# Transformer block on one core: one 512-column product for both activation parts in every transposed-output stage

## The chip, the cores and the metric

One Trainium2 chip, one of its cores. The metric is the device time of one execution in microseconds (us). Engines go by the names of the profile: PE (TensorE), with its weight loads as PEld, DVE (VectorE), ACT (ScalarE), POOL (GpSimd), SP (SyncE, which here only issues DMA).

## The reference

One block over 256 rows of width 1024, in f32. h is an RMS norm of x; `h @ w_in` (2048 columns) gives four 512-wide pieces: the input u of a pooling mixer, and q, k, v of an attention with 8 heads of 64 (RMS norm by head, rope, causal). Their outputs side by side go through `w_out` and are added to x. A second norm feeds a cross attention with 4 heads of 256 to a 256-row memory (`w_xq`, `w_xkv`, `w_xo`), added to x again. Last comes a gated feed-forward with a causal convolution of width 3:

```python
x = x + jnp.concatenate([pool, attn], axis=-1) @ w_out[l]
h = _rms_norm(x, norm_xattn_g[l]); m = _rms_norm(mem, norm_mem_g[l])
x = x + _cross_attention(h, m, w_xq[l], w_xkv[l], xq_norm_g[l], xk_norm_g[l], w_xo[l])
h = _rms_norm(x, norm_ffn_g[l])
up = h @ w_up                                   # 5632 columns: gate and val
up = sum_j conv_w[j] * shift(up, 2 - j) + conv_b
x = x + (silu(up[..., :2816]) * up[..., 2816:]) @ w_down
```

## The kernel before, in words

**Two parts for each operand.** Every f32 operand of a large product is split in a high part (ACT rounds it to f32r) and a low part (DVE subtracts the high part from the value). A product is then three products of f32r: high by high, low activation by high weight, high activation by low weight. Weights come from HBM in 62 chunks of 128 x 2048 (1 MB), each two *units* of 128 x 1024; `need(u)` issues `split_h` (ACT, `wh`, L194) and `split_l` (DVE, `wl`, L205) for units ahead of the one that PE is about to use, by `LOOKS` units (4 in most stages). Buffers are rings: `raw` 3 chunks, `wh` 7 units, `wl` 6.

**Two kinds of stage.** In `a_chunk` the activation is the stationary operand and 512 weight columns move; each 128-deep block k makes six products of 512 columns (L366, L367, L370). There are eight such chunks: k, q, v, u of `w_in` and four of `w_xkv`. The other stages give a transposed output: `b_tile` makes an output tile f of 128 features by 256 rows, with a 128 x 128 weight block as the stationary operand and the 256 activation columns moving. For each block k, `three` issues three products of 256 columns (L265, L266, L267). These stages are `w_out` (stage h1), `w_xq` (xq), `w_xo` (h2), `w_up` (up: 22 iterations i of a gate tile and a value tile) and `w_down` (down): 8 units each for the first three, 44 and 22 for the last two, so 90 units of 8 blocks, 720 calls of `three`.

**Emptying a tile.** In `resid_stage` (h1, h2) DVE adds the PSUM tile to the residual (L719), ACT writes the high part of the result times a gain (`part_h`, L250), DVE the low part (`part_l`, L256), ACT squares it (L725) and POOL sums the squares (L726). In xq the parts are made straight from PSUM. In up, `up_job` takes the two tiles of one bank: ACT writes y = conv_w[2] * tile + b (L896, two halves), DVE adds the two shifted taps (L903, four instructions), ACT Silu (L907), DVE gate times value (L909), ACT high part (L248), DVE low part (L254). In down DVE adds the residual (L946) and SP stores the tile.

**The last norm.** The first iterations of up multiply the unnormalised h2 and scale the result afterwards by r2b (L891, `SCALED` = 4 iterations). Meanwhile `r2_job` sums the squares over rows on PE (L281), makes 1/sqrt by Newton steps on POOL (`rsqrt`, L226 on DVE, then L228 to L231 three times on POOL), spreads it over partitions on PE (L869), copies it (r2b, L871, DVE) and makes hs = h2 * r2 block by block (L881, POOL), with its high part on ACT and low part on DVE. From i = 4 on PE multiplies hs.

**Rope and scores.** `rope_table` (L382, POOL) makes cos and sin times the gain of the q or k norm. `rope` on DVE multiplies with it (m1 L404, m2 L408), sums squares (L411) and adds (L413). `qk_job` then makes 1/rms of every head (`head_scale`: DVE `hk`/`hq` L243, then `rsqrt`, mostly on POOL), multiplies k by it (L431), and transposes on PE (L438). For q the scale is kept apart (`sp`, `sneg`, L445, L446, POOL) and is used in `score_job` (L530, L536).

**The order of the work** is written out by the program: jobs are generators, `tick()` advances each one by a step, and `tick()` is called after every second `three` inside `b_tile` (twice a block in `a_chunk`). `WAIT_...` lists say how many ticks a job lets pass before its next instruction is issued. Each engine then runs its own queue strictly in the order of issue, and waits where an input is not there.

Of the kernel before, what the change touches and what calls it, by code (L numbers as in the profile page):

```python
# [76 lines left out]
def block_kernel(ctx: ExitStack, tc: tile.TileContext, wpack: bass.AP, xpack: bass.AP, scal: bass.AP,  # L77
# [268 lines left out]
    xgv = tiles(pair("xg"))  # L346
# [354 lines left out]
    def b_tile(u0, f, blocks, b, mov):  # L701

        for k in range(blocks):
# [8 lines left out]
    def resid_stage(u0, actv, gain, name, phase, held):  # L712
        hv = tiles(pair(name))
        acc = t1(name + "_acc")
        for f in range(KT):
# [1 line left out]
            look[0] = HOLD[2] if f >= KT - HOLD[held] else LOOKS[phase]
            b_tile(u0, f, KT, b, lambda k: [t[:, k] for t in actv])
            dve.tensor_tensor(resid[:, f], b, resid[:, f], op=ALU.add)  # L719
            evac_split(hv[0][:, f], hv[1][:, f], resid[:, f], col(sc, gain + f))  # L720
# [24 lines left out]
    def x_job(hp):  # L745
# [56 lines left out]
    jobs_x = []  # L802
    for f in range(KT):
        b = bank()[:, 0:S]
        b_tile(34, f, KT, b, lambda k: [t[:, k] for t in h1])
        if f == 0:
            job_r1.append(go(r1_job()))
# [239 lines left out]
```

## Time and profile before

| what | value |
|---|---|
| time, three runs | 394.35, 394.62, 396.85 us; median 394.62 |
| the profiled execution | 395.07 us, span of its instructions 393.3 us |
| busy PE / DVE / ACT / POOL | 387.0 / 283.1 / 231.5 / 90.0 us |
| moved by DMA | 69.2 MB, mean 176 GB/s |

Busy time of an engine is the union of its instructions; PE's matmuls overlap one another, so the distance between two starts, not the duration of one, is what a product costs. In a timeline a row may stand for several instructions in succession (x4); the bracket is the time for which the engine sat idle before the row, and what ended that.

### The profile page before, as it was taken

To read this page: it belongs to the slowest core of one execution; us is meant where nothing else is said; L and a number is where in the kernel's file an instruction comes from. 1 tells how busy PE (TensorE), PEld (TensorE's weight loads), DVE (VectorE), ACT (ScalarE), POOL (GpSimd) and SP (SyncE) were. 2 spreads that over 40 slices of the span, in tenths; PEclk is the share of its full clock that TensorE was granted. 3 is DMA by queue.
4 is the path that set the end of the run, shared out by engine and by line. 5 is a ranking of instruction groups with operands and counts; after the bars stand their busy time and mean duration, and the time that the engine had idled before them with its cause. 6 is when DMAs were issued, how large, how long until landed. Compare 5 with 4: busy or idle time off the path is not lost.

```text
span 393.3 us, 7301 instructions
## 1 busy us (share of the span) xinstructions
PE 387.0 (98%) x2898; PEld 367.2 (93%) x2898; DVE 283.1 (72%) x478; ACT 231.5 (59%) x421; POOL 90.0 (23%) x174
## 2 busy tenths in 40 slices
PE   8999999999999999999999999999999999999996
PEld 7878787889999998899999999999999999999996
DVE  4788989956876667857774999998877874543350
ACT  5775886957476556845555498765665576342300
POOL 0384883134441423001647300000000000000000
PEclk9999999999999999999999999999999999999999
DMA  8985372543336537242545226665465452455400
GB/s 273 422 342 207 119 304 72 166 190 108 109 107 222 208 107 262 76 198 107 202 143 197 105 108 227 243 249 177 176 213 180 161 197 108 135 227 176 173 21 19
DMA packets 12274, 69.22 MB, mean 176 GB/s; under 512 B 1360, under 2 KB 2768, under 8 KB 4688
## 3 DMA queue, kind: packets, MB, share of 16 engines
q1 hardware_dynamic: 11952, 68.24, 47.9%
q8 instruction: 22, 0.36, 0.4%
q10 hardware_dynamic: 288, 0.52, 0.4%
q14 instruction: 12, 0.10, 0.1%
HBM read 67.71 MB, written 1.05 MB: 175 GB/s over the span
## 4 chain that ended last, share of the span: by engine, by line
PE 80%; DVE 7%; DMA 5%; ACT 3%; POOL 2%; issue 2%; SPq 0%; DVEq 0%; POOLq 0%
PE bank L265 23%; PE bank L267 23%; PE bank L266 23%; DMA raw<-wpack 3%; PE bank L366 3%; PE bank L367 3%; PE bank L370 3%; DVE wl L205 2%; DMA sc<-xpack 1%; ACT wh L194 1%; DVE mg_l L256 1%; ACT sqx L300 0%; PE bank L677 0%; PE bank L795 0%; POOL rs3t L228 0%
## 5 line engine op out<-in xcount | busy, mean ns | idle before, releaser
L205 DVE TENSOR_TENSOR wl<-raw,wh 128x1024 fp32r<-128x1024 f32 (+1 forms) x126 | 150.3, 1209 | 5.4 <-ACT wh L194 5.3
L194 ACT CAST wh<-raw 128x1024 fp32r<-128x1024 f32 (+1 forms) x125 | 123.7, 1024 | 41.6 <-DMA raw<-wpack 41.0
L265 PE MATMUL bank<-hs_h,wh 128*128 128x256 f32 x288 | 81.5, 283 | 0.0
L266 PE MATMUL bank<-hs_l,wh 128*128 128x256 f32 x288 | 81.5, 283 | 0.0
L267 PE MATMUL bank<-hs_h,wl 128*128 128x256 f32 x288 | 81.5, 283 | 0.0
L265 PEld LDWEIGHTS bank<-hs_h,wh 128*128 128x128 f32 x288 | 55.3, 192 | 0.0
L266 PEld LDWEIGHTS bank<-hs_l,wh 128*128 128x128 f32 x288 | 55.3, 192 | 0.0
L267 PEld LDWEIGHTS bank<-hs_h,wl 128*128 128x128 f32 x288 | 55.3, 192 | 0.0
L265 PE MATMUL bank<-act_h,wh 128*128 128x256 f32 x176 | 49.8, 283 | 0.0
L266 PE MATMUL bank<-act_l,wh 128*128 128x256 f32 x176 | 49.8, 283 | 0.0
L267 PE MATMUL bank<-act_h,wl 128*128 128x256 f32 x176 | 49.8, 283 | 0.0
L903 DVE SCALAR_TENSOR_TENSOR y<-bank,sc,y 128x255 f32<-128x255 f32 (+1 forms) x72 | 29.8, 479 | 14.4 <-ACT y L896 14.4
L265 PE MATMUL bank<-h_h,wh 128*128 128x256 f32 x128 | 36.6, 286 | 0.0
L267 PE MATMUL bank<-h_h,wl 128*128 128x256 f32 x128 | 36.2, 283 | 0.0
L266 PE MATMUL bank<-h_l,wh 128*128 128x256 f32 x128 | 36.2, 283 | 0.0
L896 ACT ACTIVATE y<-bank,sc 128x256 f32<-128x256 f32 x36 | 18.3, 559 | 27.6 <-PE bank L267 27.6
L265 PEld LDWEIGHTS bank<-act_h,wh 128*128 128x128 f32 x176 | 33.8, 192 | 0.0
L266 PEld LDWEIGHTS bank<-act_l,wh 128*128 128x128 f32 x176 | 33.8, 192 | 0.0
L267 PEld LDWEIGHTS bank<-act_h,wl 128*128 128x128 f32 x176 | 33.8, 192 | 0.0
L946 DVE TENSOR_TENSOR o<-bank,sc 128x256 f32<-128x256 f32 x8 | 3.4, 425 | 35.2 <-PE bank L267 35.2
L366 PE MATMUL bank<-wh,mg_h 128*128 128x512 f32 x64 | 26.1, 408 | 0.0
L726 POOL TENSOR_TENSOR h_acc<-h_sq,h_acc 128x256 f32<-128x256 f32 x14 | 16.8, 1198 | 40.3 <-ACT h_sq L725 40.2
(244 smaller groups left out, 862.4 us busy)
## 6 DMA issues: line engine op xcount, KB each, us to landing
raw<-wpack SPq DMA_DIRECT2D x59, 1024.0 KB, 4.8
raw<-wpack SPq DMA_DIRECT2D x4, 512.0 KB, 7.7
mraw<-memT SPq DMA_DIRECT2D x4, 256.0 KB, 7.7
out<-o SPq DMA_DIRECT2D x8, 128.0 KB, 1.9
raw<-wpack ACTq DMA_DIRECT2D x2, 256.0 KB, 3.7
raw<-wpack SPq DMA_DIRECT2D x2, 256.0 KB, 4.7
sc<-xpack SPq DMA_DIRECT2D x1, 512.0 KB, 6.0
tab<-table SPq DMA_DIRECT2D x1, 480.0 KB, 9.7
```

The source lines that it names most:

```text
L194: copy(split[u][0][:, r], unit(u)[:, r])
L205: dve.tensor_tensor(l[:, r], unit(u)[:, r], h[:, r].bitcast(F32), op=ALU.subtract)
L256: dve.scalar_tensor_tensor(l, src, scale, h.bitcast(F32), op0=ALU.mult, op1=ALU.subtract)
L265: pe.matmul(o, stat[0], mov[0], start=start, stop=False)
L266: pe.matmul(o, stat[0], mov[1], start=False, stop=False)
L267: pe.matmul(o, stat[1], mov[0], start=False, stop=stop)
L366: pe.matmul(bk[tt], a[tt][0], wv[0], start=k == 0, stop=False)
L367: pe.matmul(bk[tt], a[tt][1], wv[0], start=False, stop=False)
L370: pe.matmul(bk[tt], a[tt][0], wv[1], start=False, stop=k == KT - 1)
L726: pool.tensor_tensor(acc, sq, acc, op=ALU.add)
L896: act.activation(y[:, g * S:(g + 1) * S], src[:, g * S:(g + 1) * S], AF.Identity, bias=col(sc, C_CB + f), scale=col(sc, C_CW + 2 * 2 * NFF ...
L903: dve.scalar_tensor_tensor(yy[:, j:], uu[:, :S - j], col(sc, C_CW + (2 - j) * 2 * NFF + f), yy[:, j:], op0=ALU.mult, op1=ALU.add)
```

## The change

1. The high and low part of an activation lie side by side in one tile: for every block 256 high and then 256 low columns (`pair`, `tiles`). In `b_tile` the call of `three` becomes `both`: one product of the high weight with all 512 columns, and one of the low weight with the 256 high columns. Columns 0 to 255 of the PSUM bank then hold two of the three terms, columns 256 to 511 the third, and a tile fills a whole bank instead of half of one.
2. Whoever empties a tile adds the two halves: two DVE adds in `resid_stage` and down; in xq and in up an ACT copy of the second half to SBUF and a DVE add of the first. In up this is done for each of the two tiles of an iteration, so that everything behind it reads SBUF.
3. In `resid_stage` and xq the low part is issued two ticks later (`WAIT_LOW`), except for the last tile, where it comes at once.
4. `r2_job`: the Newton steps run on DVE in nine instructions instead of twelve on POOL (`quick`), its waits are shorter (`WAIT_R2`), and hs is used from i = 3 (`SCALED`).
5. The rope table of k is made on POOL behind the sum of squares of x instead of ahead of it; the f32r copies of the identity and the mask go from POOL to ACT; q's head scale is issued ahead of q's transposes instead of behind them; three more waits change (`WAIT_POOL`, `WAIT_KEY`, `WAIT_R1`).

```diff
-WAIT_POOL = [1, 6, 0, 7, 1, 5, 2, 6, 1]
-WAIT_KEY = [0, 4, 7, 2, 0, 13, 5]
-WAIT_R1 = [0]
+WAIT_POOL = [1, 6, 0, 7, 1, 5, 2, 2, 1]
+WAIT_KEY = [0, 8, 7, 2, 0, 13, 5]
+WAIT_R1 = [6]
...
-WAIT_R2 = [6, 11, 2, 2, 0]
+WAIT_R2 = [6, 6, 1, 1, 0]
+WAIT_LOW = [2]
...
-SCALED = 4
+SCALED = 3
...
     def pair(name, cols=KT * S):
-        h = pairs.tile([P, cols], F32R, name=name + "_h", tag="ph", bufs=4)
-        l = pairs.tile([P, cols], F32R, name=name + "_l", tag="pl", bufs=4)
-        return h, l
+        return pairs.tile([P, 2 * cols], F32R, name=name, tag="pair", bufs=4)
...
         for _ in range(3):
+            if quick:
+                dve.tensor_tensor(t, y, y, op=ALU.mult)
+                dve.scalar_tensor_tensor(t, t, -0.5, x, op0=ALU.mult, op1=ALU.mult)
+                dve.scalar_tensor_tensor(y, t, 1.5, y, op0=ALU.add, op1=ALU.mult)
+                continue
...
+    def both(b, stat, mov, start, stop):
+        n = mov.shape[1] // 2
+        if start:
+            pe.matmul(b, stat[0], mov, start=True, stop=False)
+            pe.matmul(b[:, 0:n], stat[1], mov[:, 0:n], start=False, stop=False)
+        else:
+            pe.matmul(b[:, 0:n], stat[1], mov[:, 0:n], start=False, stop=False)
+            pe.matmul(b, stat[0], mov, start=False, stop=stop)
...
     def late_constants():
-        pool.tensor_copy(identr, ident)
-        pool.tensor_copy(maskr[:, 0:2 * P], tab[:, T_MASK:T_MASK + 2 * P])
+        act.copy(identr, ident)
+        act.copy(maskr[:, 0:2 * P], tab[:, T_MASK:T_MASK + 2 * P])
...
-        if n == "k":
-            while "ex" not in rows:
-                yield
-            s = head_scale("hk", ssq["k"], HEADS, HD, rows["ex"])
+        while "ex" not in rows:
+            yield
+        s = head_scale("h" + n, ssq[n], HEADS, HD, rows["ex"])
+        if n == "q":
+            pool.tensor_scalar(sp, s, HD ** -0.5, None, op0=ALU.mult)
+            pool.tensor_scalar(sneg, s, -(HD ** -0.5), None, op0=ALU.mult)
+        else:
...
-        yield from row_stat("x", lambda k: resid[:, k], lambda: rope_table("q", T_GQ, T_GQS))
+        def tables():
+            rope_table("k", T_GK, T_GKS)
+            rope_table("q", T_GQ, T_GQS)
+
+        yield from row_stat("x", lambda k: resid[:, k], tables)
         late_constants()
-    rope_table("k", T_GK, T_GKS)
...
-            three(b, wv, mov(k), k == 0, k == blocks - 1)
+            both(b, wv, mov(k), k == 0, k == blocks - 1)
...
+        def empty(f, b):
+            for z in range(2):
+                dve.tensor_tensor(resid[:, f], b[:, z * S:(z + 1) * S], resid[:, f], op=ALU.add)
+            g = col(sc, gain + f)
+            part_h(hv[0][:, f], resid[:, f], g)
...
+            if f < KT - 1:
+                yield from wait(WAIT_LOW[0])
+            part_l(hv[1][:, f], resid[:, f], hv[0][:, f], g)
...
-        part_h(xqv[0][:, f], b, col(ggx, f % 2))
-        part_l(xqv[1][:, f], b, xqv[0][:, f], col(ggx, f % 2))
+    def xq_empty(f, b):
+        q = t1(f"xq{f}")
+        act.copy(q, b[:, S:])
+        dve.tensor_tensor(q, b[:, 0:S], q, op=ALU.add)
+        g = col(ggx, f % 2)
+        part_h(xqv[0][:, f], q, g)
...
-        r2 = rsqrt(v2, TT)
+        r2 = rsqrt(v2, TT, True)
...
-    def up_job(i, b, scaled):
-        src = b
+    def up_job(i, bs, scaled):
+        src = t2(f"up{i}")
+        for g in range(2):
+            half = src[:, g * S:(g + 1) * S]
+            act.copy(half, bs[g][:, S:])
+            dve.tensor_tensor(half, bs[g][:, 0:S], half, op=ALU.add)
...
-        b = bank()[:, 0:S]
+        b = bank()
         b_tile(102, f, NFF, b, act_tile)
         o = t2(f"o{f}")[:, 0:S]
-        dve.tensor_tensor(o, b, resid[:, f], op=ALU.add)
+        for z, add in enumerate((resid[:, f], o)):
+            dve.tensor_tensor(o, b[:, z * S:(z + 1) * S], add, op=ALU.add)
```

What the change does to the order shows at three places. The first is DVE in the middle of up, one iteration long (`up`, `y` and `sg` are tiles of up, `wl` is the low part of a weight unit, `act` the activation for down). Before:

```order
L903 SCALAR_TENSOR_TENSOR y_2958<-bank_2888,sc,y_2958 128x255 x2
L903 SCALAR_TENSOR_TENSOR y_2958<-bank_2888,sc,y_2958 128x254 x2
L205 TENSOR_TENSOR wl_2998<-raw_2780,wh_2962 128x1024
L909 TENSOR_TENSOR sg_2944<-sg_2944,y_2885 128x256
L254 TENSOR_TENSOR act_l<-sg_2799,act_h 128x256
L205 TENSOR_TENSOR wl_3035<-raw_2851,wh_2996 128x1024
```

And now, in the changed kernel:

```order
L929 TENSOR_TENSOR up_2895<-bank_2842,up_2895 128x256
L929 TENSOR_TENSOR up_2895<-bank_2843,up_2895 128x256
L205 TENSOR_TENSOR wl_2907<-raw_2745,wh_2870 128x1024
L945 SCALAR_TENSOR_TENSOR y_2900<-up_2895,sc,y_2900 128x255 x2
L945 SCALAR_TENSOR_TENSOR y_2900<-up_2895,sc,y_2900 128x254 x2
L205 TENSOR_TENSOR wl_2933<-raw_2745,wh_2905 128x1024
L951 TENSOR_TENSOR sg_2885<-sg_2885,y_2839 128x256
L259 TENSOR_TENSOR act_2311<-sg_2762,act_2311 128x256
```

Two adds have come in, with one weight unit between them and the taps that read what ACT makes of their result.

The second place is DVE where the normalised activation hs is finished and the work on up is taken up again. Before (the last two of eight low parts of hs, and what follows):

```order
L256 SCALAR_TENSOR_TENSOR hs_l<-hs_2632,sc,hs_h 128x256
L256 SCALAR_TENSOR_TENSOR hs_l<-hs_2636,sc,hs_h 128x256
L903 SCALAR_TENSOR_TENSOR y_2582<-up_2580,sc,y_2582 128x255 x2
L903 SCALAR_TENSOR_TENSOR y_2582<-up_2580,sc,y_2582 128x254 x2
L903 SCALAR_TENSOR_TENSOR y_2587<-up_2585,sc,y_2587 128x255 x2
L903 SCALAR_TENSOR_TENSOR y_2587<-up_2585,sc,y_2587 128x254 x2
L891 TENSOR_TENSOR up_2666<-bank_2553,r2b 128x512
L205 TENSOR_TENSOR wl_2674<-raw_2442,wh_2598 128x1024
```

And now:

```order
L261 SCALAR_TENSOR_TENSOR hs_2245<-hs_2381,sc,hs_2245 128x256
L261 SCALAR_TENSOR_TENSOR hs_2245<-hs_2385,sc,hs_2245 128x256
L261 SCALAR_TENSOR_TENSOR hs_2245<-hs_2389,sc,hs_2245 128x256
L945 SCALAR_TENSOR_TENSOR y_2354<-up_2312,sc,y_2354 128x255 x2
L945 SCALAR_TENSOR_TENSOR y_2354<-up_2312,sc,y_2354 128x254 x2
L929 TENSOR_TENSOR up_2405<-bank_2317,up_2405 128x256
L929 TENSOR_TENSOR up_2405<-bank_2318,up_2405 128x256
L934 TENSOR_TENSOR up_2405<-up_2405,r2b 128x512
L205 TENSOR_TENSOR wl_2418<-raw_2246,wh_2344 128x1024
```

`wl_2674` is unit 68 of the weights, `wl_2418` unit 66: up begins with unit 58 and uses two units an iteration, so before the last low part issued ahead of hs is that of unit 67, for the second tile of i = 4, and now that of unit 65, for the second tile of i = 3. Between r2b and hs there stand two scalings of up and one weight unit before, and one scaling and no weight unit now.

The third place is the head of POOL's queue. Before:

```order
L382 TENSOR_TENSOR ropek<-tab 128x128 x2
L301 TENSOR_TENSOR accx<-sqx_190,accx 128x256
L301 TENSOR_TENSOR accx<-sqx_199,accx 128x256
L301 TENSOR_TENSOR accx<-sqx_214,accx 128x256
L301 TENSOR_TENSOR accx<-sqx_223,accx 128x256
```

And now (the last three of the seven adds, then the tables):

```order
L320 TENSOR_TENSOR accx<-sqx_232,accx 128x256
L320 TENSOR_TENSOR accx<-sqx_241,accx 128x256
L320 TENSOR_TENSOR accx<-sqx_256,accx 128x256
L401 TENSOR_TENSOR ropek<-tab 128x128 x2
L401 TENSOR_TENSOR ropeq<-tab 128x128 x2
```

The table of k, which stood ahead of all seven adds, stands behind them, with the table of q. DVE's own order does not change there: its first product with `ropek` stands at the same place in its queue, ahead of the same weight units.

## Rows read from the trace of the kernel before

**Rows 1.** The page, part 1: busy time, share of the span, instructions.

```profile
PE 387.0 (98%) x2898; PEld 367.2 (93%) x2898; DVE 283.1 (72%) x478; ACT 231.5 (59%) x421; POOL 90.0 (23%) x174
```

**Rows 2.** Waits of PE from 10 us on: total us, times, longest.

```profile
PE bank L621 <- DVE ul L256: 0.6, 1, 0.6
PE bank L265 <- DVE cat_l L256: 0.4, 1, 0.4
PE bank L281 <- POOL accx L301: 0.3, 1, 0.3
```

**Rows 3.** Line 265: count, durations, first and last start.

```profile
L265 PE MATMUL bank<-hs_h,wh x288: 283/283/283, 222.6 to 325.9; 128*128 128x256 f32 x144
```

**Rows 4.** Timeline of PE in a chunk of w_xkv: start us, us.

```profile
158.08 0.39 PE L366 MATMUL bank<-wh,mg_h 128*128 128x512 f32 x1
...
160.80 0.39 PE L366 MATMUL bank<-wh,mg_h 128*128 128x512 f32 x1
```

**Rows 5.** Timeline of PE where 256-column and 512-column products meet.

```profile
61.80 0.28 PE L624 MATMUL bank<-maskr,ul 128*128 128x256 f32 x1
61.92 0.40 PE L366 MATMUL bank<-wh,mg_h 128*128 128x512 f32 x1
62.16 0.39 PE L367 MATMUL bank<-wh,mg_l 128*128 128x512 f32 x1
```

**Rows 6.** Windows in h2, early up: us busy PE, PEld, DVE, ACT, POOL; PEclk, DMA.

```profile
180.00:200.00 20.00, 20.00 (x169) 20.00 (x168) 13.49 (x21) 11.20 (x21) 8.69 (x6) 1.00 0.45 159
222.00:264.00 42.00, 42.00 (x352) 42.00 (x351) 41.19 (x74) 31.37 (x53) 0.00 (x0) 1.00 0.50 178
```

**Rows 7.** Timeline of DVE, one iteration in the middle of up.

```profile
275.71 1.65 DVE L903 SCALAR_TENSOR_TENSOR y<-bank,sc,y 128x255 f32<-128x255 f32 x4 [1.17 <-ACT y L896]
277.28 1.22 DVE L205 TENSOR_TENSOR wl<-raw,wh 128x1024 fp32r<-128x1024 f32 x1
...
281.47 1.65 DVE L903 SCALAR_TENSOR_TENSOR y<-bank,sc,y 128x255 f32<-128x255 f32 x4 [1.17 <-ACT y L896]
```

**Rows 8.** Timeline of DVE in down: add from PSUM, next instruction.

```profile
334.42 0.42 DVE L946 TENSOR_TENSOR o<-bank,sc 128x256 f32<-128x256 f32 x1 [3.20 <-PE bank L267]
334.76 1.22 DVE L205 TENSOR_TENSOR wl<-raw,wh 128x1024 fp32r<-128x1024 f32 x1
```

**Rows 9.** Timeline of ACT in the middle of up.

```profile
274.66 1.02 ACT L896 ACTIVATE y<-bank,sc 128x256 f32<-128x256 f32 x2 [2.23 <-PE bank L267]
```

**Rows 10.** Groups by line: an ACT copy of 256 columns from PSUM.

```profile
L552 ACT COPY pt<-bank 128x256 f32<-128x256 f32 x4 | 1.3, 389 | 0.0
```

**Rows 11.** Timeline of DVE from 204 us: the last norm and the hand-over.

```profile
204.27 0.15 DVE L284 TENSOR_SCALAR v<-bank 128x2 f32<-128x2 f32 x1
...
212.02 0.42 DVE L871 COPY r2b<-bank 128x256 f32<-128x256 f32 x1 [2.76 <-PE bank L869]
...
221.48 3.24 DVE L903 SCALAR_TENSOR_TENSOR y<-up,sc,y 128x255 f32<-128x255 f32 x8
...
225.23 1.21 DVE L205 TENSOR_TENSOR wl<-raw,wh 128x1024 fp32r<-128x1024 f32 x1
```

**Rows 12.** Timeline of POOL: hs block by block.

```profile
212.53 7.16 POOL L881 TENSOR_TENSOR hs<-sc,r2b 128x256 f32<-128x256 f32 x8 [1.83 <-DVE r2b L871]
```

**Rows 13.** Timeline of PE: the first product of up.

```profile
198.70 0.28 PE L265 MATMUL bank<-h_h,wh 128*128 128x256 f32 x1
```

**Rows 14.** Timeline of POOL from 15 us: table of k, sum of squares.

```profile
15.77 2.19 POOL L382 TENSOR_TENSOR ropek<-tab 128x128 f32<-128x128 f32 x2 [15.35 <-DMA tab<-table]
...
19.94 6.58 POOL L301 TENSOR_TENSOR accx<-sqx,accx 128x256 f32<-128x256 f32 x5 [0.46 <-ACT sqx L300]
```

**Rows 15.** Timeline of DVE from 23 us: rope of k, its scaling.

```profile
23.51 1.29 DVE L404 TENSOR_TENSOR m1k<-bank,ropek 128x512 f32<-128x512 f32 x2 [1.09 <-ACT sqk L403]
...
39.98 1.29 DVE L431 TENSOR_TENSOR m1k<-m1k,rs1y 128x512 f32<-128x512 f32 x2 [1.80 <-POOL rs1y L231]
```

**Rows 16.** Timeline of PE: transposes of k.

```profile
40.76 1.28 PE L438 MATMUL bank<-tab,m1k 128*128 128x128 f32 x8
```

More of the change, by code (lines that the diff above doesn't have):

```diff
@@ L345, in block_kernel @@
     nc.sync.dma_start(sc[:, C_GMEM:], scal)
-    xgv = tiles(pair("xg"))
+    xgv = tiles(pair("xg"), KT, S)
     def first_splits():
@@ L363, in a_chunk @@
             wv = [t[:, (k % 2) * 512:(k % 2) * 512 + 512] for t in w]
-            a = [[t[:, k, tt * P:(tt + 1) * P] for t in actv] for tt in range(TT)]
+            a = [[t[:, k, tt * P:(tt + 1) * P] for t in actv[:2]] for tt in range(TT)]
             for tt in range(TT):
@@ L487, in mem_job @@
             part_l(mgv[1][:, k], r, mgv[0][:, k], col(sc, C_GMEM + k))
-    mgv = tiles(pair("mg"))
+    mgv = tiles(pair("mg"), KT, S)
     job_v = go(v_job())
@@ L592, in block_kernel @@
     a_chunk(12, xgv, bu)
-    cat = tiles(pair("cat"))
+    cat = tiles(pair("cat"), KT, S)
     def pool_job():
@@ L689, in block_kernel @@
     finish(job_k)
-    kxv = tiles(pair("kx"))
+    kxv = tiles(pair("kx"), KT, S)
     job_key0 = go(key_job(0, bk0))
@@ L712, in resid_stage @@
     def resid_stage(u0, actv, gain, name, phase, held):
-        hv = tiles(pair(name))
+        hv = tiles(pair(name), KT, S)
         acc = t1(name + "_acc")
-        for f in range(KT):
-            b = bank()[:, 0:S]
[L717 to L720, printed above, removed]
+        def empty(f, b):
[3 more added lines that the diff above has]
+            part_h(hv[0][:, f], resid[:, f], g)
             if f == 0:
@@ L726, in resid_stage @@
                 pool.tensor_tensor(acc, sq, acc, op=ALU.add)
+            if f < KT - 1:
+                yield from wait(WAIT_LOW[0])
+            part_l(hv[1][:, f], resid[:, f], hv[0][:, f], g)
+        for f in range(KT):
+            b = bank()
+            look[0] = HOLD[2] if f >= KT - HOLD[held] else LOOKS[phase]
+            b_tile(u0, f, KT, b, lambda k: actv[2][:, k])
+            go(empty(f, b))
             tick()
@@ L731, in block_kernel @@
     h1, acc1 = resid_stage(26, cat, C_GX, "h1", 6, 0)
-    xqv = tiles(pair("xq"))
+    xqv = tiles(pair("xq"), KT, S)
     sqp = {}
@@ L753, in x_job @@
                 for dd in range(2):
-                    q = [t[:, 2 * h + dd, tt * P:(tt + 1) * P] for t in xqv]
-                    three(o, q, [t[:, 2 * h + dd] for t in kxv], dd == 0, dd == 1)
+                    q = [t[:, 2 * h + dd, tt * P:(tt + 1) * P] for t in xqv[:2]]
+                    three(o, q, [t[:, 2 * h + dd] for t in kxv[:2]], dd == 0, dd == 1)
             if tt == 0:
@@ L788, in x_job @@
         if not ptv:
-            ptv.extend(t.rearrange("p (h m q) -> p h m q", h=XH, m=TT) for t in pair("xpt"))
+            ptv.extend(tiles(pair("xpt"), XH, TT, S))
         for j, h in enumerate(hs):
@@ L800, in x_job @@
         yield from wait(WAIT_X[7])
[L802 to L807, printed above, removed]
-        part_h(xqv[0][:, f], b, col(ggx, f % 2))
-        part_l(xqv[1][:, f], b, xqv[0][:, f], col(ggx, f % 2))
+    def xq_empty(f, b):
[4 more added lines that the diff above has]
+        part_h(xqv[0][:, f], q, g)
         sq = t1(f"xsq{f}")
-        act.activation(sq, b, AF.Square)
+        act.activation(sq, q, AF.Square)
         if f % 2 == 0:
@@ L815, in block_kernel @@
             pool.tensor_tensor(sqp[f // 2], sq, sqp[f // 2], op=ALU.add)
+        if f < KT - 1:
+            yield from wait(WAIT_LOW[0])
+        part_l(xqv[1][:, f], q, xqv[0][:, f], g)
+    jobs_x = []
+    for f in range(KT):
+        b = bank()
+        b_tile(34, f, KT, b, lambda k: h1[2][:, k])
+        if f == 0:
+            job_r1.append(go(r1_job()))
+        go(xq_empty(f, b))
         tick()
@@ L836, in block_kernel @@
     a_chunk(42, mgv, bv0)
-    vxv = [t.rearrange("p (m d) -> p m d", m=TT) for t in pair("vx")]
+    vxv = tiles(pair("vx"), TT, XH * XD)
     go(value_job(0, bv0))
@@ L840, in block_kernel @@
     a_chunk(46, mgv, bv1)
-    oxv = tiles(pair("ox"))
+    oxv = tiles(pair("ox"), KT, S)
     finish(*jobs_x)
@@ L848, in block_kernel @@
             for mt in range(TT):
-                v = [t[:, mt, h * XD + dd * P:h * XD + (dd + 1) * P] for t in vxv]
-                three(o, v, [t[:, h, mt] for t in ptv], mt == 0, mt == TT - 1)
+                v = [t[:, mt, h * XD + dd * P:h * XD + (dd + 1) * P] for t in vxv[:2]]
+                three(o, v, [t[:, h, mt] for t in ptv[:2]], mt == 0, mt == TT - 1)
         evac_split(oxv[0][:, 2 * h:2 * h + 2], oxv[1][:, 2 * h:2 * h + 2], b.rearrange("p (d s) -> p d s", d=2))
@@ L910, in up_job @@
         yield from wait(WAIT_UP[4])
-        h, l = (t[:, i % 8] for t in acts[i // 8])
+        h, l = (t[:, i % 8] for t in acts[i // 8][:2])
         part_h(h, sg[:, S:])
@@ L919, in block_kernel @@
     for i in range(NFF):
-        b = bank()
+        bs = [bank(), bank()]
         if i == 0:
-            hs2 = tiles(pair("hs2"))
+            hs2 = tiles(pair("hs2"), KT, S)
             job_r2.append(go(r2_job()))
@@ L932, in block_kernel @@
         if i % 8 == 0:
-            acts.append(tiles(pair(f"act{i // 8}")))
-        jobs_up.append(go(up_job(i, b, scaled)))
+            acts.append(tiles(pair(f"act{i // 8}"), KT, S))
+        jobs_up.append(go(up_job(i, bs, scaled)))
         tick()
```

28 lines of the change are left out of this document (13 added, 15 removed).

## Prediction

> **What bounds the kernel now.** I read the page's busy times first, then PE's list of waits, then PE's timeline for the price of one product, and DVE's and ACT's timelines for the room that they have. PE is busy for 98% of the span [rows 1], and from 10 us on it waits for other engines for 0.6 + 0.4 + 0.3 = 1.3 us in all [rows 2]. So the time is the number of products times the distance between two starts. DVE, at 72%, comes second, but not evenly: in 42 us of early up it is busy for 41.2 [rows 6]. Both things have to be kept in view: what PE gains, and whether DVE can follow.
>
> **Term 1: the products.** In up, 288 blocks of three products start from 222.6 to 325.9: 103.3 / 287 = 0.360 us a block, 0.120 a product of 256 columns [rows 3]. In a chunk, 12 products of 512 columns lie between 158.08 and 160.80: 0.227 each [rows 4]. Twice 0.120 is 0.240, so a product carries about 0.013 that does not grow with its columns. The change puts 0.227 + 0.120 = 0.347 in place of 0.360. There are 90 units of 8 blocks, 720 in all: 720 x 0.013 = 9.4 us less. No row shows the two forms alternating for long; where they meet once, the 256-column product takes 0.12 and the 512-column one 0.24 [rows 5], which would leave no gain at all (0.36). At the other end, if the shorter product cost only what 256 more columns cost (0.227 - 0.120 = 0.107), the gain is 720 x 0.026 = 18.7. I take 9.4, since each form then keeps the price of its own long run, and 0.24 is a single case.
>
> The Trainium skill (TensorE: Matmul & The Clock Gate, Back-to-back issue gap) speaks against this term: it gives 262 cycles for 256 columns and 518 for 512, so that merging two products saves 6 cycles, 2.5 ns at 2.4 GHz (PE's granted clock is 1.00 in the windows [rows 6]). By that page the term would be an estimated 720 x 2.5 ns = 1.8 us. The trace does not agree with its figures: 0.120 instead of 0.109 for 256 columns, 0.227 instead of 0.216 for 512. I weigh it as a rival below, worked out from rows.
>
> **Term 2: the adds.** Outside up they lie beside PE. In h2 DVE is busy for 13.5 and ACT for 11.2 of 20 us [rows 6]; one more DVE add for a tile is 0.34 (L946 to the next start [rows 8]) in 2.8 us. If that cover were gone, 24 tiles would cost 8 us. In down DVE waits 3.2 us ahead of such an add [rows 8]. Only the very last add has no cover: +0.35 at the end.
>
> In up an iteration has 16 blocks, 5.76 us before and 16 x 0.347 = 5.55 after. DVE's timeline repeats every 5.76 with 1.17 of waiting [rows 7], so it works for 4.59. Two adds bring 0.68: 5.27, and 0.28 is left. DVE becomes almost as full as PE, but does not bound. ACT waits 2.23 in an iteration [rows 9]; two copies at 0.39 [rows 10] fit in. The new round trip is add (0.42), then two ACT activations (1.02 [rows 9]), then the taps; one weight unit (1.22 [rows 7]) stands between the add and the taps, so the taps wait for at most some 0.2, and only when DVE is not late anyway. I take nothing here; what it costs if it doesn't hold is the last rival.
>
> **Term 3: the hand-over to hs.** Here DVE is late. Before, r2b is copied at 212.02, 13.3 us after up begins [rows 11, 13]; hs takes POOL until 219.7 [rows 12], DVE is through with the low parts at 221.5, and the first weight unit behind them starts at 225.23 and ends at 226.4 [rows 11]. That unit is 68. PE begins hs with unit 66 at 222.6 [rows 3], so it needs 68 two units, 5.76 us, later: at 228.4, 2.0 to spare.
>
> Now the Newton steps take ten short DVE operations in place of POOL's; I put them at 0.2 each, an estimate from v's 0.15 [rows 11] and a short pause between dependent ones. The row mean v came 5.6 after up began [rows 11, 13]; with one more add ahead of it 5.9, then 2.0 for Newton, 0.7 for the adds of i = 0, two weight units 2.3: r2b at about 11.0. From r2b, eight blocks on POOL at 0.9 [rows 12] and one ACT and one DVE piece, about 1.0: 8.3. Then four taps 1.57 [rows 7], two adds 0.7, a scaling 0.6, and the unit 1.2: ready at 11.0 + 8.3 + 4.1 = 23.4. That unit is 66 now. PE needs it for i = 4, behind 4 x 5.55 = 22.2, the small products 0.9 (222.62 less 198.70 less four times 5.76) and the first 512 columns 0.23: at 23.3. So the 2 us are used up. With PE moving at 5.55 and DVE at 5.27, each later iteration gives 0.28 back, so it is paid once. I take 0.8, with ends 0 and 4 (each piece above may be half as long again as the row).
>
> **Term 4: the first 90 us.** There are no calls of `three` on activation tiles here but the moved work. Taking q's scale ahead of its transposes and the two f32r copies off POOL lets `sneg` come earlier, which DVE's maximum step waits for ahead of `ul`; PE's waits for `ul` and `cat_l`, 1.0 us [rows 2], can go. The copies on ACT cost nothing that anyone waits for there: ACT is at 59% [rows 1].
>
> The rope table goes the other way. Before it is made from 15.77, and the last of the squares' adds ends at 19.94 + 6.58 = 26.5 [rows 14]. Now it stands behind them. The last add loses the weight unit beside it and may end at 25.5; half the table then takes 0.8. DVE's m1k, at 23.51 so far [rows 15], can start at about 26.3, 2.8 later, and it blocks four weight units, the sums of squares of k and hk. The scaling of k is at 39.98 [rows 15], and PE's transposes start at 40.76 [rows 16], 0.1 after its first half is done: no slack. I let 2.2 of the 2.8 reach PE: 2.2 - 1.0 = +1.2, with ends -1.3 (all of rows 2 gone, nothing lost) and +3.0.
>
> **Sum**, from the profiled execution, 395.07: -9.4 + 0.35 + 0.8 + 1.2 = -7.05, so 388.0. The median of the runs is 0.45 lower (394.62), so the forecast is 387.6.
>
> **Rivals.** *The early part is all gain.* If the tables cost PE nothing, term 4 is -1.3 and term 3 zero: 395.07 - 9.4 + 0.35 - 1.3 = 384.7, on the median's scale 384.3. For it: PE's few waits there [rows 2]; against it: the start of the transposes [rows 16] right behind the scaling. If the products' term is larger too, towards 12, 381.7.
>
> *The hand-over becomes a stall.* Unit 66 and the ones behind it come late by 4 us instead of 0.8: 390.8. For it: DVE busy for 98% of 42 us before the change adds to it [rows 6]; against it: the 2.0 spare in the old order.
>
> *The products do not get cheaper.* If the alternation costs what the single meeting shows [rows 5], or the fixed part is not saved, term 1 is 0 and PE leaves DVE more time, so term 3 is 0: 395.07 + 0.35 + 1.2 = 396.6, on the median's scale 396.2. Against it: 0.120 and 0.227 in hundreds of products [rows 3, 4]. By the Trainium skill's page above, an estimated 1.8 less, 394.4, which is this case too.
>
> *Slower: DVE's queue sets the pace of up.* The mechanism is the round trip DVE add, ACT copy and y, DVE tap in one strictly ordered queue. If DVE keeps its 1.17 of waiting in each iteration [rows 7], because it now waits for the copy as well as for y, an iteration takes 4.59 + 0.68 + 1.17 = 6.44, not 5.55: 19 iterations on hs x 0.89 = 16.9, and 387.2 (without term 3) + 16.9 = 404.1, on the median's scale 403.7. The point from which this decides: 5.55 + 7.85 / 19 = 5.96 us an iteration is no gain. For it: those waits are for ACT now. Against it: they end when PE ends a tile, so a late DVE doesn't have them, and the weight unit stands in the gap.
>
> **How the numbers follow.** Chances: forecast 0.58; early part all gain 0.17; hand-over 0.13; products no cheaper 0.06; DVE the bound 0.06. Within 1%, about what a measurement of this kernel can tell from no change, means 390.7 to 398.6. Faster: all of the first two but a few hundredths, and nearly half of the hand-over, 0.78; same: the rest of these and the products' rival, 0.16; slower 0.06. The range goes from 381.5 (gain on both early part and products) to 392.6 (term 3 at 4, term 4 at 3: 395.07 - 9.4 + 0.35 + 4 + 3 = 393.0, less 0.45); the forecast's own is 385 to 390.5.
>
> **What would show it.** Term 1: the same 103 us of hs blocks, now 38 x 8 = 304 blocks of two products, at 0.347 each; 0.36 makes it wrong. Term 2: DVE nearly without waits in up and PE without any from i = 5 on; a PE list of waits with `wl` in every iteration would be the last rival. Term 3: one wait of PE at the first block of unit 66, under 2 us. Term 4: m1k near 26.3 instead of 23.5, a new wait of PE at the transposes of k, and none at `ul`. A time above 393 or below 381 would mean that one of these is not the mechanism.

## The result and the profile after

The changed kernel takes 390.87 us (median of four runs, 390.23 to 391.86) and the kernel before 394.81 beside it: a ratio of 0.989, 95% interval 0.987 to 0.991. That is 3.9 us less, where 7.0 were forecast; 387.6 lies 3.3 us below the measurement. The profiled execution took 390.8, with a span of 389.0 (before 393.3).

The page of the changed kernel, busy times (answers to [rows 1]):

```profile
PE 381.3 (98%) x2178; PEld 328.7 (84%) x2178; DVE 313.3 (81%) x562; ACT 248.2 (64%) x475; POOL 77.1 (20%) x160
```

PE still fills its span, with 720 products fewer. DVE has gained 30 us of work.

PE's waits from 5 us on, changed kernel (total, times, longest; answers to [rows 2]):

```profile
PE bank L460 <- DVE m1k L453: 1.4, 1, 1.4
PE bank L279 <- DVE wl L205: 1.0, 1, 1.0
```

The three small waits of [rows 2] are gone, and two new ones stand in their place: at the transposes of k (L460), and at the first low weight of a unit (L279), which is in up.

Windows of whole stages: w_xo, up from the first product on hs, down (us busy PE, PEld, DVE, ACT, POOL; then PEclk, DMA share, GB/s). Before:

```profile
175.66:198.70 23.04, 23.04 (x194) 23.04 (x193) 15.55 (x23) 12.90 (x22) 8.69 (x6) 1.00 0.39 138
222.62:326.30 103.68, 103.68 (x867) 103.68 (x866) 89.94 (x160) 69.32 (x117) 0.00 (x0) 1.00 0.52 184
326.30:389.54 63.24, 63.24 (x530) 63.24 (x528) 27.05 (x35) 19.37 (x23) 0.00 (x0) 1.00 0.36 130
```

After (up has 304 blocks on hs here, 288 before):

```profile
174.72:197.09 22.37, 22.37 (x130) 19.50 (x129) 19.50 (x30) 12.92 (x22) 4.39 (x6) 1.00 0.38 142
214.76:322.92 108.16, 107.07 (x609) 92.39 (x608) 106.60 (x206) 84.84 (x163) 0.88 (x2) 1.00 0.51 185
322.92:384.69 61.77, 61.77 (x353) 53.67 (x351) 32.20 (x47) 20.09 (x26) 0.00 (x0) 1.00 0.37 134
```

The length of a window divided by its blocks is the price of a block: 23.04 / 64 = 0.360 before and 22.37 / 64 = 0.3495 now in w_xo; 0.360 and 108.16 / 304 = 0.3558 on hs, where PE also waits. The window of down ends where its last product starts, so the price of that product (0.12 before, 0.23 now) is added: 63.36 / 176 = 0.360 and 62.00 / 176 = 0.3523. All at a granted clock of 1.00.

With the same stage bounds, read from PE's timeline, the 4.3 us of the two spans divide as follows. "Forecast" is the forecast's own term by stage (its 0.013 a block, its terms 2 to 4), "at 0.3495" what the blocks alone would give:

| stage (blocks) | before | after | difference | forecast | at 0.3495 |
|---|---|---|---|---|---|
| start to w_out | 90.36 | 90.25 | -0.11 | +1.2 | 0 |
| w_out (64) | 24.42 | 23.76 | -0.66 | -0.83 | -0.67 |
| w_xq and first scores (64) | 27.68 | 27.50 | -0.18 | -0.83 | -0.67 |
| cross attention | 33.20 | 33.21 | 0 | 0 | 0 |
| w_xo (64) | 23.04 | 22.37 | -0.67 | -0.83 | -0.67 |
| up (352) | 127.60 | 125.83 | -1.77 | -4.6 + 0.8 | -3.70 |
| down (176), with its last product | 63.36 | 62.00 | -1.36 | -2.3 | -1.85 |
| behind the last product | 3.63 | 4.10 | +0.46 | +0.35 | 0 |

Two products of w_xo, PE's timeline of the changed kernel (start us, us):

```profile
184.64 0.39 PE L282 MATMUL bank<-ox,wh 128*128 128x512 f32 x1
184.87 0.27 PE L281 MATMUL bank<-ox,wl 128*128 128x256 f32 x1
184.98 0.40 PE L282 MATMUL bank<-ox,wh 128*128 128x512 f32 x1
```

The 512-column product holds PE for 0.23 and the 256-column one for 0.11 to 0.12 (medians of the distances to the next start, over all blocks: 233 and 117 ns; in down 236 and 118). The forecast had 227 and 120.

DVE's timeline, one iteration in the middle of up (answers to [rows 7]):

```profile
272.42 0.74 DVE L929 TENSOR_TENSOR up<-bank,up 128x256 f32<-128x256 f32 x2
273.08 1.21 DVE L205 TENSOR_TENSOR wl<-raw,wh 128x1024 fp32r<-128x1024 f32 x1
274.21 1.66 DVE L945 SCALAR_TENSOR_TENSOR y<-up,sc,y 128x255 f32<-128x255 f32 x4
275.79 1.22 DVE L205 TENSOR_TENSOR wl<-raw,wh 128x1024 fp32r<-128x1024 f32 x1
276.93 0.42 DVE L951 TENSOR_TENSOR sg<-sg,y 128x256 f32<-128x256 f32 x1
...
277.60 0.75 DVE L929 TENSOR_TENSOR up<-bank,up 128x256 f32<-128x256 f32 x2
```

No row has a wait: the 1.17 us of [rows 7] are filled. The pattern repeats after 277.60 - 272.42 = 5.18 us, faster than PE's 16 x 0.3495 = 5.59, so DVE never stops: it is working off what it was behind.

It was behind since the hand-over to hs. DVE there (bracket: idle before, and what ended it):

```profile
222.31 1.22 DVE L205 TENSOR_TENSOR wl<-raw,wh 128x1024 fp32r<-128x1024 f32 x1
225.03 0.76 DVE L929 TENSOR_TENSOR up<-bank,up 128x256 f32<-128x256 f32 x2 [1.50 <-ACT up L928]
225.82 0.69 DVE L934 TENSOR_TENSOR up<-up,r2b 128x512 f32<-128x512 f32 x1
226.43 1.22 DVE L205 TENSOR_TENSOR wl<-raw,wh 128x1024 fp32r<-128x1024 f32 x1
```

and ACT, whose copy DVE waits for:

```profile
219.72 1.09 ACT L938 ACTIVATE y<-up,sc 128x256 f32<-128x256 f32 x2 [3.00 <-DVE up L934]
220.72 1.03 ACT L194 CAST wh<-raw 128x1024 fp32r<-128x1024 f32 x1
221.77 1.28 ACT L949 ACT_TABLE_LOAD   x1
223.07 0.42 ACT L949 ACTIVATE sg<-y 128x256 f32<-128x256 f32 x1
223.39 1.03 ACT L194 CAST wh<-raw 128x1024 fp32r<-128x1024 f32 x1
224.33 0.41 ACT L949 ACTIVATE sg<-y 128x256 f32<-128x256 f32 x1
224.64 0.62 ACT L928 COPY up<-bank 128x256 f32<-128x256 f32 x2
```

The weight unit at 226.43 is number 68. PE has reached it:

```profile
226.36 0.39 PE L278 MATMUL bank<-hs,wh 128*128 128x512 f32 x1
227.70 0.38 PE L279 MATMUL bank<-hs,wl 128*128 128x256 f32 x1 [0.96 <-DVE wl L205]
```

From 226.36 to 227.70 is 1.34, where 0.23 is the rule. Smaller delays stand ahead of units 66 and 69: over their unit's eight blocks 0.38 and 0.27 us, and 1.20 for 68. ACT came to the hand-over with 3.00 us of waiting behind it, and then had its table to load at the one place where DVE depends on the copy behind it.

At the end of the kernel DVE has two adds behind the last product:

```profile
385.12 0.42 DVE L989 TENSOR_TENSOR o<-bank,sc 128x256 f32<-128x256 f32 x1 [5.74 <-PE bank L282]
385.57 0.42 DVE L989 TENSOR_TENSOR o<-bank,o 128x256 f32<-128x256 f32 x1
```

In the early part POOL now makes the table of k at 25.30 behind the seven adds, and DVE waits for it:

```profile
25.80 1.29 DVE L423 TENSOR_TENSOR m1k<-bank,ropek 128x512 f32<-128x512 f32 x2 [3.49 <-POOL ropek L401]
...
41.71 1.30 DVE L453 TENSOR_TENSOR m1k<-m1k,rs1y 128x512 f32<-128x512 f32 x2 [1.80 <-POOL rs1y L236]
```

m1k is 2.3 us later than in [rows 15] and the scaling 1.7. PE's transposes start at 42.46 instead of 40.76 [rows 16]:

```profile
42.46 1.32 PE L460 MATMUL bank<-tab,m1k 128*128 128x128 f32 x8 [1.44 <-DVE m1k L453]
```

Yet w_out begins no later (90.25, before 90.36).

### The profile page after: what moved, and what is told of

Read it like the earlier page. It is cut to its first block, busy times and chain, and to the rows that moved or that the text cites. A ratio compares the mean times of both kernels' runs of the same rounds, so it can differ in the third digit from the quotient of the medians.

```text
span 389.0 us, 5984 instructions
## 1 busy us (share of the span) xinstructions
PE 381.3 (98%) x2178; PEld 328.7 (84%) x2178; DVE 313.3 (81%) x562; ACT 248.2 (64%) x475; POOL 77.1 (20%) x160
## 4 chain that ended last, share of the span: by engine, by line
PE 79%; DVE 9%; DMA 3%; ACT 3%; issue 2%; POOL 2%; SPq 0%; DVEq 0%
PE bank L282 34%; PE bank L281 17%; PE bank L385 5%; PE bank L386 5%; PE bank L389 5%; PE bank L278 4%; DVE wl L205 3%; PE bank L279 2%; DMA raw<-wpack 2%; DVE hs L261 2%; DMA sc<-xpack 1%; PE bank L272 1%; PE bank L271 1%; PE bank L270 1%; ACT wh L194 1%
## 5 line engine op out<-in xcount | busy, mean ns | idle before, releaser
L282 PE MATMUL bank<-hs,wh 128*128 128x512 f32 x266 | 94.8, 396 | 0.0
L281 PE MATMUL bank<-hs,wl 128*128 128x256 f32 x266 | 74.2, 279 | 0.0
L282 PE MATMUL bank<-act,wh 128*128 128x512 f32 x168 | 59.6, 398 | 0.0
L282 PEld LDWEIGHTS bank<-hs,wh 128*128 128x128 f32 x266 | 49.9, 188 | 10.3
L281 PEld LDWEIGHTS bank<-hs,wl 128*128 128x128 f32 x266 | 50.1, 189 | 1.6
L281 PE MATMUL bank<-act,wl 128*128 128x256 f32 x168 | 47.1, 281 | 0.0
L945 DVE SCALAR_TENSOR_TENSOR y<-up,sc,y 128x255 f32<-128x255 f32 (+1 forms) x88 | 36.6, 477 | 0.3 <-ACT y L938 0.3
L282 PE MATMUL bank<-h,wh 128*128 128x512 f32 x98 | 35.1, 396 | 0.0
L385 PE MATMUL bank<-wh,mg 128*128 128x512 f32 x64 | 26.1, 408 | 0.0
L385 PE MATMUL bank<-wh,xg 128*128 128x512 f32 x64 | 26.0, 406 | 0.0
L386 PE MATMUL bank<-wh,xg 128*128 128x512 f32 x64 | 25.4, 397 | 0.0
L386 PE MATMUL bank<-wh,mg 128*128 128x512 f32 x64 | 25.1, 392 | 0.0
```

Source lines behind the costliest of these rows:

```text
L281: pe.matmul(b[:, 0:n], stat[1], mov[:, 0:n], start=False, stop=False)
L282: pe.matmul(b, stat[0], mov, start=False, stop=stop)
L385: pe.matmul(bk[tt], a[tt][0], wv[0], start=k == 0, stop=False)
L386: pe.matmul(bk[tt], a[tt][1], wv[0], start=False, stop=False)
L945: dve.scalar_tensor_tensor(yy[:, j:], uu[:, :S - j], col(sc, C_CW + (2 - j) * 2 * NFF + f), yy[:, j:], op0=ALU.mult, op1=ALU.add)
```

## The experiments

Three questions were open: whether the Silu table or DVE's load makes unit 68 late; whether the table of k costs 1.7 us or nothing; and why a block costs 0.350 and not 0.347.

**The Silu table loaded early.** One instruction more in `r2_job`, where ACT has time:

```diff
         r2 = rsqrt(v2, TT, True)
+        act.activation(sm("warm_silu", TT), v2, AF.Silu)
         yield from wait(WAIT_R2[1])
```

> The changed kernel (390.87 us) with one more ACT instruction, a Silu of two columns behind the row mean of the last norm, so that ACT loads its table there, where it has 3 us of idle time, and not in the chain of the first scaled iteration. Theory A: the 1.28 us load in ACT's queue is what makes ACT's copies of iteration 3 late, DVE's add wait 1.50 us, and weight unit 68 late by 1.2 us on PE. Then DVE's wait falls to about 0.2, PE's wait at unit 68 goes, at unit 69 too: 389.2 to 389.7. Rival B: DVE is simply too full behind the hand-over (the low parts of hs, four taps, adds, scalings), and the load only fills time in which DVE would be late anyway: PE still waits 0.8 or more at unit 68, time 390.6 to 391.1.

Measured: 390.21 us (389.04 to 390.73). ACT's and DVE's timelines of this kernel:

```profile
201.53 1.28 ACT L905 ACT_TABLE_LOAD   x1
202.95 0.20 ACT L905 ACTIVATE warm_silu<-v 128x2 f32<-128x2 f32 x1
```

```profile
221.95 1.22 DVE L205 TENSOR_TENSOR wl<-raw,wh 128x1024 fp32r<-128x1024 f32 x1
223.25 0.76 DVE L930 TENSOR_TENSOR up<-bank,up 128x256 f32<-128x256 f32 x2
```

DVE goes from the weight unit to the adds with 0.08 us between, and the list of PE's waits has nothing of up any more (unit 66 still costs 0.36): the 304 blocks on hs take 106.74 instead of 108.17 us, 1.43 less. So theory A holds in the profile. The median, 0.66 us under the changed kernel's, shows less than half of it and lies between the two ranges. This kernel's runs differ in the granted clock (mean 1.000 in the run of 389.80, 0.995 and 0.993 in those of 390.73 and 390.62), and a loss of that kind shows in the early part of a kernel below; that it hides the gain here is not shown, since only the run of 389.04 (0.997) has a trace.

The Trainium skill (ScalarE: Activation LUTs, What ACT_TABLE_LOAD costs) gives 1283 ns for a load, as the row has it, and 1380 ns more to drain for every switch; the rows here don't show that part: Silu starts 0.02 us behind the load at 221.77.

**hs from iteration 4 again.**

```diff
-SCALED = 3
+SCALED = 4
```

> The changed kernel with hs used from iteration 4 again (SCALED = 4), nothing else. Theory A: hs stands at the same place in DVE's queue, so nothing comes earlier; one more scaling of up (0.69 us on DVE) comes in: units 68 to 70 as late as now or later, 390.9 to 391.7. Rival B: using hs one iteration earlier is what made the hand-over late; with a whole iteration more (5.6 us) PE has no wait in up: 388.9 to 389.3.

Measured: 391.14 us. PE's wait at L279 stands at 1.0 as before. Theory A: the earlier use of hs is not what makes the hand-over late.

**The table of k ahead of the sums.**

```diff
         def tables():
-            rope_table("k", T_GK, T_GKS)
             rope_table("q", T_GQ, T_GQS)
...
+    rope_table("k", T_GK, T_GKS)
     stat_x = go(stat_job())
```

> The changed kernel with the rope table of k made ahead of the squares' sums again, all other moved work as it is. Theory A (term 4 as forecast): the wait of PE at the transposes of k, 1.6 us, is a loss of its own; m1k starts near 23.5, PE's transposes near 40.8, and nothing later takes it back: 389.1 to 389.5. Rival B: the 1.7 us are absorbed, since PE waited later in the early part for other chains (ul, cat_l) in the kernel before, which now end with time to spare because PE is late: with PE early these waits return in part and the mixer's parts start at the same 90.3 us: 390.6 to 391.0.

Measured: 388.60 us (388.37 to 389.59), 0.9845 of the kernel before (0.9825 to 0.9864), a little under theory A's range. DVE's first product of the rope and PE's transposes:

```profile
22.90 1.29 DVE L423 TENSOR_TENSOR m1k<-bank,ropek 128x512 f32<-128x512 f32 x2 [0.81 <-ACT sqk L422]
```

```profile
40.47 1.05 PE L460 MATMUL bank<-tab,m1k 128*128 128x128 f32 x8
```

The wait at the transposes is gone, and PE's only wait left is the one in up, 0.9. w_out begins at 87.96, 2.29 us earlier than in the changed kernel and 2.40 earlier than in the kernel before. So theory A: the move costs 2.3 us that nothing takes back, and the changed kernel spends on it the 2.4 that are saved elsewhere. Not all of the 2.4 is shown to be the other moves' work: the kernel without any moves, below, begins w_out at 90.00, which leaves them some 2.0.

**Products of two blocks grouped.**

```diff
-            both(b, wv, mov(k), k == 0, k == blocks - 1)
+            if k % 2 == 0:
+                held = (wv, mov(k))
+            else:
+                (w0, m0), (w1, m1) = held, (wv, mov(k))
+                pe.matmul(b, w0[0], m0, start=k == 1, stop=False)
+                pe.matmul(b, w1[0], m1, start=False, stop=False)
+                pe.matmul(b[:, 0:S], w0[1], m0[:, 0:S], start=False, stop=False)
+                pe.matmul(b[:, 0:S], w1[1], m1[:, 0:S], start=False, stop=k == blocks - 1)
```

> The changed kernel with the products of two blocks grouped: two of 512 columns, then two of 256. Now 512 is followed by 256 after 233 ns and 256 by 512 after 117: 350 a block, where the forecast put 227 + 120 = 347. Theory A: a form keeps the price of its long run where its neighbour is of the same form; half of the meetings are then alike and a block costs 347 or less, 720 x 3 ns = 2 us less: 388.5 to 389.2. Rival B: the price is not set by the neighbour (it is that of writing half of a bank, or of the columns themselves): 350 a block, 390.6 to 391.1.

Measured: 391.20 us, which by the time alone is nearest to rival B. PE's timeline in down:

```profile
349.98 0.40 PE L732 MATMUL bank<-act,wh 128*128 128x512 f32 x1
350.21 0.40 PE L733 MATMUL bank<-act,wh 128*128 128x512 f32 x1
350.45 0.28 PE L734 MATMUL bank<-act,wl 128*128 128x256 f32 x1
350.56 0.27 PE L735 MATMUL bank<-act,wl 128*128 128x256 f32 x1
350.68 0.40 PE L732 MATMUL bank<-act,wh 128*128 128x512 f32 x1
```

A 512-column product takes 0.23 ahead of another of its kind too (median 233 ns; 235 ahead of one of 256 columns), so it does not come down to 227 beside its own kind; theory A's reason falls. Yet a block does cost less: 22.29 / 64 = 0.3483 in w_xo, where it cost 0.3495, and 61.31 / 176 = 0.3484 in down with its last product, where it cost 0.3523. In w_xo it is the 256-column products that are cheaper (mean 115 ns instead of 116); in down also those of 512 columns (233 instead of 236), for a reason that no run shows. The time didn't show it because the early part lost 2.4 us, and windows there show to what:

```profile
42.00:44.00 2.00, 0.74 (x5) 0.54 (x6) 1.53 (x3) 1.50 (x5) 1.67 (x6) 1.00 0.87 356
44.00:46.00 2.00, 2.00 (x9) 1.67 (x10) 2.00 (x5) 1.92 (x5) 1.67 (x5) 0.67 0.35 147
46.00:48.00 2.00, 2.00 (x7) 1.52 (x6) 2.00 (x5) 2.00 (x5) 1.57 (x6) 0.50 0.00 0
```

Behind the wait for the transposes of k (1.72 us of idle PE, transposes from 43.22) the granted clock fell to half, the 1.2 GHz level, and the 18 products behind the transposes took 5.80 us instead of the 4.20 of the changed kernel. In the profiled run of the changed kernel the same wait, 1.44, left the clock at 1.00.

**The parts of the change alone.** Products, adds and later low parts without the moved work, and the moved work on the kernel before:

```diff
-WAIT_R2 = [6, 6, 1, 1, 0]
+WAIT_R2 = [6, 11, 2, 2, 0]
...
-SCALED = 3
+SCALED = 4
...
-        r2 = rsqrt(v2, TT, True)
+        r2 = rsqrt(v2, TT)
```

(and every other line of points 4 and 5 undone likewise; the second kernel has exactly these lines of the change and no others.)

> The kernel before with the products, the adds and the later low parts alone (points 1 to 3 of the change), none of the moved work (points 4 and 5). From the stages of the changed kernel: products 720 x 0.0105 = 7.6 us less, 0.5 lost in xq, 0.4 in down, 0.5 at the end: 388.9 to 389.3 where the hand-over to hs has no wait. Theory A: the hand-over of the old order (Newton on POOL, hs from iteration 4) has no room for the adds and for the Silu table either, and PE waits there as in the changed kernel or longer: 390.5 to 392.5. Rival B: the 2 us to spare in the old order hold: 388.9 to 389.5; then the moves around the last norm brought the wait.

> The kernel before with the moved work alone (points 4 and 5), products of 256 columns as before. Theory A: the moved table costs the 1.7 to 2.3 us that it costs in the changed kernel, the rest of the moves in the early part gives the same back (PE's waits at ul and ahead of w_out go), and up has no wait to lose: 394.5 to 395.5. Rival B: the moves give a gain of their own, 1 us or more, which the changed kernel loses elsewhere: under 394.

Measured: 391.95 us (0.9924, 0.9909 to 0.9939) for the products alone, 395.36 (1.0018, 1.0005 to 1.0031) for the moves alone. PE's waits in the first:

```profile
PE bank L279 <- DVE wl L205: 2.0, 3, 1.2
PE bank L643 <- DVE ul L261: 0.5, 1, 0.5
PE bank L278 <- DVE cat L261: 0.4, 1, 0.4
```

and in the second:

```profile
PE bank L446 <- DVE m1k L439: 2.2, 1, 2.2
```

Theory A both times. The products alone bring 3.1 us. The old hand-over has no room for the adds: units 68, 70 and 71 are late by 0.79, 1.46 and 0.63 us, 2.9 in all against 1.9 in the changed kernel, with the same table load in ACT's queue. That difference of 1.0 is what point 4 adds to the products' gain in the changed kernel. The moves alone bring nothing: what they save at `ul` and ahead of w_out they spend at the transposes.

**The mends together.** Table of Silu early and table of k first; then the same with grouped products.

> The changed kernel with both mends, the Silu table early and the rope table of k ahead of the sums. They lie 180 us apart. Theory A: they add, 1.4 and 2.3 us: 386.9 to 387.5. Rival B: a PE that is 2.3 us earlier meets weights or DVE later in up, and one of the two is lost: 388.2 to 389.

> The same with the products of two blocks grouped. In the grouped kernel a block took 0.3477 us in down and 0.3483 in w_xo, instead of 0.3509 and 0.3495, and its early part lost 2.5 us to a wait and to the lower clock level behind it. Theory A: without that wait the early loss goes, and the blocks' 1.2 to 1.4 us show in the time: 385.5 to 386.2. Rival B: what was lost early is a cost of the grouping, or DVE at 60 of 60 us in up takes the gain: 386.9 to 387.6.

Measured: 387.53 us for the two (386.95 to 387.72; the expected end was 387.5, so they add within what runs differ by), and 385.43 for all three (385.19 to 385.49), 0.9758 of the kernel before (0.9742 to 0.9774): theory A. (The expectation's two prices for down leave out the last product; with it they are 0.3484 and 0.3523.) This version is faster than both kernels. Windows of its three stages:

```profile
172.10:194.40 22.30, 22.30 (x131) 19.46 (x130) 19.47 (x30) 12.90 (x22) 4.37 (x6) 1.00 0.38 143
212.01:318.21 106.20, 106.20 (x610) 92.26 (x609) 106.05 (x205) 82.93 (x160) 0.91 (x2) 1.00 0.53 188
318.21:379.41 61.20, 61.20 (x354) 53.38 (x352) 32.73 (x48) 20.66 (x28) 0.00 (x0) 1.00 0.38 137
```

On hs 106.20 / 304 = 0.3493 a block, with PE busy in all of it and DVE in 106.05 of 106.20: a full DVE costs PE next to nothing here (units 66 and 69 are late by 0.19 and 0.09) as long as its queue isn't held up.

**Which moves saved the early 2.4 us, and what point 4 is worth.** Three kernels, each the best one with a part undone: q's scale behind its transposes; the f32r copies on POOL; point 4 (Newton steps, waits, `SCALED`) as before.

> The kernel of all three mends (385.43 us) with q's head scale issued behind q's transposes again. It splits the 2.4 us that the moved work without the table of k gives back before w_out. Theory A (the forecast's): sneg comes late again, DVE's maximum step waits for it ahead of ul, PE waits at ul and behind it at the parts of the mixer, all of it, 1.2 + 0.7 us: 387.0 to 387.6. Rival B: POOL without the two f32r copies is fast enough, and the scale's place matters little: 385.2 to 385.9.

> The kernel of all three mends with the f32r copies of the identity and the mask on POOL again. Theory A (it is the place of q's scale that counts): 385.2 to 385.9. Rival B: POOL's queue is what sneg waits in, so the copies bring back the waits at ul and ahead of w_out, 1 us or more: 386.4 to 387.6.

> The kernel of all three mends with the last norm as before: Newton steps on POOL, its longer waits, hs from iteration 4. Theory A: with the Silu table loaded early the old order has room, its 2 us to spare hold, and point 4 of the change is worth under 0.5 us: 385.2 to 386.0. Rival B: r2b comes 4 us later and DVE has four taps and two scalings more behind hs, so units 68 and 70 are late without the table load too: 386.6 to 388.

Measured: 387.23, 385.67 and 387.12 us. The place of q's scale is worth 1.8 us by the medians, as theory A has it, but the profile shows only one of its two waits. With the scale late DVE waits 1.9 us for `sneg` (0.7 with it early), and PE waits for `ul` again:

```profile
DVE nbs L552 <- POOL sneg L465: 1.9, 1, 1.9
```

```profile
PE bank L643 <- DVE ul L261: 0.3, 1, 0.3
```

w_out begins 1.2 us later, of 1.55 between the two profiled runs; the other 0.4 lies behind the last product, where the scale has no part. PE does not wait at the parts of the mixer, where the products alone waited, and neither undone part brings that wait back: it may be the three changed waits (`WAIT_POOL`, `WAIT_KEY`, `WAIT_R1`) that took it away, which no run tried. The copies are worth 0.2, no more than runs differ by. Point 4 is worth 1.7 us even with the table early: rival B. In its profile units 68, 70 and 71 are late by 0.56, 0.15 and 0.60 us (the rival named 68 and 70), and in down PE loses another 0.63 in the third unit, where it waits for `act`.

## Why the prediction was right in its direction and too large in its size

The direction held. The time, 390.87, lies above the forecast's own 385 to 390.5 and just inside the band from 390.7 to 398.6, within which the prediction gave "same" a chance of 0.16. It is also the rival number for a hand-over that becomes a stall, 390.8, but by chance: that rival puts 4 us on the hand-over, and 1.9 were lost there.

**Term 1, products: right mechanism, too large.** This is the step that failed most: "each form then keeps the price of its own long run". 720 x 0.0105 = 7.6 us in place of 9.4, and down's blocks, at 0.3523, give 0.5 less still. The 512-column product costs 233 ns in these stages (236 in down), not the 227 of the chunks [rows 4], also beside its own kind; the 256-column one 117, not 120 [rows 3]. The forecast's split in columns and a fixed part does not hold: 233 is twice 117 within a nanosecond. What makes 512 columns dearer here than in the chunks, and dearer still in down, stays open. By the table of the Trainium skill (TensorE: Matmul & The Clock Gate, Back-to-back issue gap), an estimated 2.5 ns a block would have been saved. The runs show 10.5, so weighing the rows higher than the page was right.

**Term 2, adds: right.** Behind the hand-over DVE is without waits in up, at 5.18 an iteration for 5.27, and does not bound. The end grew by 0.46, not 0.35: the second add starts 0.45 behind the first. One cost was not seen: w_xq gains 0.18 instead of 0.67. At the end of w_out two adds for the last tile stand ahead of the next weight unit on DVE, and PE is late at that unit's first low product (from 116.83 to 117.35); that the adds are the reason is read from the queue, no run tried it.

**Term 3, hand-over: right place, wrong reason and size.** Unit 66 is late, as forecast, by 0.38 us (0.8 forecast). But the step "with PE moving at 5.55 and DVE at 5.27, each later iteration gives 0.28 back, so it is paid once" failed: unit 68, the first of i = 5, from which on PE was to have no wait, is late by 1.20, because DVE's adds wait for ACT's copies, which stand behind a 1.28 us table load. The forecast counted DVE's queue there and not ACT's. In all 1.9 us instead of 0.8. The early load removes 1.43 of it, so that mechanism is shown. The old norm (2.9 with the products alone) shows that point 4 was needed: the "2.0 to spare" were gone with the adds.

**Term 4, early part: both halves found, the balance wrong.** The table of k cost what was forecast (2.2 forecast; 2.29 by undoing it), m1k at 25.8 for 26.3, with the new wait at the transposes. But 2.4 came back, not 1.0 (some 2.0 of it by the moves): -0.1 in place of +1.2. "PE's waits for `ul` and `cat_l`, 1.0 us" took the list of waits at its word, whereas the lost time between PE's starts was 0.76 + 0.20 at `ul` and 0.22 + 0.61 ahead of w_out. And both were put down to `sneg`; undoing q's scale brought back `ul` alone.

The sum, in the profiled executions (395.07 to 390.8): products 1.8 us less than forecast, down 0.5, hand-over 1.1, w_xq 0.5, the end 0.1, and 1.3 more in the early part: 2.7 of the 7.05 did not come.

## What to carry to other kernels

When a wait is moved into a chain that passes through two engines, read both queues up to that point: an engine with 3 us of idle time ahead can still be late if a one-time cost, such as a table load, stands between the idle time and the instruction that is waited for. A product's price from another stage is an estimate for the new one: here 0.227 became 0.233, and 6 ns in each of 720 blocks outweighed the 3 ns by which the 256-column product came out cheaper. And take a change apart: here one of its moves cost 2.3 us, more than half of what the whole change brought, and the list of waits named it.

## What was not expected of the hardware

A wait of PE of 1.4 to 2.2 us can cost more than itself: in the grouped kernel it was followed by some 3.4 us at the granted clock's lower level (0.67, 0.50 and 0.98 in the windows from 44 to 50 us), 1.6 us lost, with a mean clock of 0.995 in all four runs of that kernel. In the profiled run of the moves alone the same wait, 2.24, left the clock at 1.00; two of that kernel's ten runs had a mean clock of 0.995, and they took 396.60 and 397.07 us, against a median of 395.36. What decides whether the clock falls stays open. Also, PE's weight loads were busy for 23.04 of 23.04 us in w_xo before and for 19.50 of 22.37 now: with products of 256 columns alone they followed one another without a break. Whether this set the old 120 ns was not tried.
